# One GLA block, then two diffusion-transformer layers on one core: modulation loads on another queue, two-step ends of the feed-forward's pairs, residuals by tile, a later output step

## The chip, the cores and the metric

The kernel runs on one core of one Trainium2 chip. The metric is the device time of one execution in microseconds (us), the median of several runs. Engine names: PE is TensorE (matmuls, whose weight loads are shown as PEld), DVE is VectorE, ACT is ScalarE, POOL is GpSimd, SP is SyncE, whose queue issues most of the loads from memory.

## What is computed

A first block of 256 tokens of width 1024 (gated linear attention, then a squared-ReLU feed-forward) makes x. Two layers follow on x (the latent tokens) and on 256 context tokens. Each layer takes six modulation vectors from a condition vector: shift, scale and gate for its attention and for its feed-forward. Layer 0 (neighbourhood attention) updates latent and context tokens; layer 1 (grouped-query attention with rotary positions) only the latent ones.

```python
for i in range(DEPTH_2):                       # 2
    ctx_out = i < DEPTH_2 - 1
    mod_l = (silu_c @ ada_w[i] + ada_b[i])[:, None, :]
    mod_c = (silu_cc @ ada_w[i] + ada_b[i])[None, None, :]
    ...
    a_l = ada_norm(h, norm_mix[i], sh1_l, sc1_l)
    a_c = ada_norm(hc, norm_mix[i], sh1_c, sc1_c)
    ...                                        # y_l, y_c: the layer's attention
    h = h + g1_l * y_l
    h = h + g2_l * swiglu_ffn(ada_norm(h, norm_ffn[i], sh2_l, sc2_l), ffn_w_in[i], ffn_w_out[i])
    if ctx_out:
        hc = hc + g1_c * y_c
        hc = hc + g2_c * swiglu_ffn(ada_norm(hc, norm_ffn[i], sh2_c, sc2_c), ffn_w_in[i], ffn_w_out[i])
return rms_norm_2(h, norm_final)

def swiglu_ffn(h, w_in, w_out):
    a, g = jnp.split(h @ w_in, 2, axis=-1)
    return (jax.nn.silu(a) * g) @ w_out
```

The hidden width of the feed-forward is 2816, 22 tiles of 128. `ada_w` of one layer is a matrix of 1024 by 6 x 1024.

## The kernel before

**Weights and products.** Every product is made in about fp32 precision from three matmuls (`mm3`, L213 to L215): each operand is split into a high part, a rounded copy (`wh` or `h`), and a low part, the rest (`wl` or `l`). A weight tile of 128x1024 (512 KB) is loaded by SP's queue into one of five `raw` buffers (`w_load`, L157), then split by ScalarE (copy, L194) and VectorE (subtraction, L195); `wnext` hands out the next one and keeps a few tiles split ahead (`cap`). The order of all weight tiles is the list `UNITS`.

**Modulation.** The products with the condition vector are not made on TensorE. `ada_jobs` (L318) walks over steps, each a 512 KB tile of `ada_w`: it is loaded into one of two buffers `a` (L333) and multiplied and summed along its rows on VectorE with the broadcast condition vector (L353), twice where latent and context tokens both need it. After eight steps GpSimd adds the bias (L368). There are four such walks. `adaC` is the only one with an `order` (the list `STEPS`): its 48 steps cover the feed-forward gate of layer 0 and most of layer 1's modulation, and its steps are taken one or two at a time between the tiles of layer 0's feed-forward (`ada_next`, L1313).

**Layer 0's feed-forward** works on 512 tokens, four token tiles (0 and 1 latent, 2 and 3 context), and on its 22 hidden tiles in four parts (`PARTS`). For each hidden tile f the up products are made, and after each part the down products (`ffn_down0`). Fourteen of the hidden tiles (`SEVEN`) are made as a pair of token halves with seven products in place of eight (`ffn_up7`, L1255): products of sums of tokens (`sT`) with sums of weights. The sums of weights are made while the tile before is worked on (`pair_sums`, L1217, a generator with four pieces; L1230, L1231 split them, L1236 to L1246 add them on VectorE). In `ffn_up7` TensorE accumulates on r, q and g. r is copied out by ScalarE after the first product (L1275), q after the second (L1277), r again after the third (L1284) and after the next product on r (L1291); TensorE may go on accumulating on r only after each copy. `step(cut)` runs the next piece of `pair_sums` behind the copy given.

**The end of a tile.** The last operations on a tile's activations, `end`, are held back if the next tile is a pair, and run in that pair behind the copy of q (L1278 to L1281). For an ordinary tile, `end` splits the product (L1157 on ScalarE, L1158 on VectorE). For a pair it takes silu of the second half (L1305, ScalarE), multiplies (L1306, VectorE) and splits (L1307 ScalarE, L1308 VectorE).

**Down products and residuals.** The last part's down products (`ffn_down0_last`, L1364) are made for half the columns and two token tiles at a time. Then `gated` (L1111) multiplies each of the two tiles by its gate (L1113) and adds it to the residual (L1114), both on VectorE. The squares, the root and the norm of the rows follow (L231 ScalarE, L224 VectorE, L225 GpSimd, L243 VectorE), and the transposes into layer 1 (L258, L271 to L276).

**Layer 1's attention** makes 32 units (16 heads by 2 query tiles), staged: in each step n of the loop one unit is started (scores L1676, L1677) and older ones are moved on (softmax L1682 to L1691, transposes L1695, values L1709). `qfill(n)` (L1728) puts other work between: the rest of the projections and, from `oproj`, one step of the output projection, of its residual and of its transposes. Every n takes one step of `oproj` except n = 29. What is left runs after the loop.

**What sets the order.** At the start and at the end of the kernel the order on some engines is the order written. In between, instructions are put in order when the program is made, by the place in the text and by what is ready; `tc.issue_after(x)` makes the instructions written inside it, on x's engine, follow x. Each engine and queue then works strictly in that order.

Of the kernel before, what the change touches and what calls it, by code (L numbers as in the profile page):

```python
# [15 lines left out]
ALU = mybir.AluOpType  # L16
# [74 lines left out]
def net(ctx, tc, x, xt, small, gk_up, gk_b, g_onorm, wst, final_norm, ctx_in, ctx_t, ada, ada_b, cvec,  # L91
# [226 lines left out]
    def ada_jobs(jobs, order=None):  # L318

        steps = [(L, v, both, k) for L, v, both in jobs for k in range(KD)]  # L320
        if order is not None:
            two, one = [z for z in steps if z[2]], [z for z in steps if not z[2]]
            steps = [(two if n == "2" else one).pop(0) for n in "".join(order)]
            assert not two and not one
        loaded = {}

        def load(n):
            if n < len(steps):
                L, v, _, k = steps[n]
                loaded[n] = sb.tile([P, D], F32, tag="ada", bufs=2, name=nm("a"))  # L330
                if (L, v) == (0, 0) and k < 2:
                    G.tensor_copy(out=loaded[n][:, 0:1], in_=crow[k][:, 0:1])
                nc.sync.dma_start(out=loaded[n], in_=ada[(L * 6 + v) * KD + k])  # L333

        later = []

        def advance():
            for z in list(later):
                if z[0] < site[0]:
                    z[0] = site[0]  # L340
                    if next(z[1], "end") == "end":
                        later.remove(z)

        for n, (L, v, both, k) in enumerate(steps):
            if n == 0:
                load(0)
            load(n + 1)
            raw = loaded.pop(n)
            n_c = 2 if both else 1
            for ci in range(n_c):  # L350
                if k == 0:
                    modc[(L, ci, v)] = const([P, KD], nm("mod"))
                V.tensor_tensor_reduce(out=raw if ci == n_c - 1 else t2([D], BF16), in0=raw, in1=crow[ci], scale=1.0,  # L353
                                       scalar=0.0, op0=ALU.mult, op1=ALU.add,
                                       accum_out=modc[(L, ci, v)][:, k:k + 1])
            if k == KD - 1:
                later.append([site[0], ada_finish(L, v, n_c)])
            yield advance
        while later:
            site[0] += 1  # L360
            advance()
            yield advance
# [748 lines left out]
    def gated(res, acs, L, ci, v, hf):  # L1111
        tmp = t2([512])
        V.tensor_tensor(out=tmp, in0=acs, in1=gates[(L, ci, v, hf)], op=ALU.mult)  # L1113
        V.tensor_tensor(out=res[hf], in0=tmp, in1=res[hf], op=ALU.add)  # L1114

    hc = ctx_tiles()
    run(steps, 100)
# [28 lines left out]
    def ffn_act(pa, pg_, n, hold=False):  # L1146
        a = t2([n])
        A.activation(out=a, in_=pa[:, :n], func=AF.Silu)
        V.tensor_tensor(out=a, in0=pg_[:, :n], in1=a, op=ALU.mult)  # L1149
        if n > S:  # L1150
            h, l = t2([n], F32R), t2([n], F32R)
        else:
            z = t2([2, n], F32R)
            h, l = z[:, 0, :], z[:, 1, :]

        def end():
            A.copy(out=h, in_=a)  # L1157
            V.tensor_tensor(out=l, in0=a, in1=h, op=ALU.subtract)  # L1158

        held_ends.append(end) if hold else end()  # L1160
        return h, l

    def ffn_up(L, src, n, conv=iter(()), hold=False):
# [91 lines left out]
    def ffn_up7(got, conv, hold):  # L1255
        wpos[2] += 2
        r, q, g = [bank()[:, 0:S] for _ in range(3)]
        c1, c2, c3 = t2([2, S]), t2([2, S]), t2([2, S])
        H = KD // 2

        def prod(o, n, c, X, first=True):
            h, l = got[n]
            for j in range(H):
                k = slice(c + j * P, c + (j + 1) * P)
                mm3(o, h[:, k], l[:, k], *X(j), first and j == 0, j == H - 1, not first)

        def step(cut):
            with tc.issue_after(cut.ins):
                run(conv)

        def a(t, j):
            return xs(fT, j, S * t, S)

        prod(r, 0, 0, lambda j: a(0, j))
        A.copy(out=c1[:, 0, :], in_=r)  # L1275
        prod(q, 1, 0, lambda j: sT[(3, j)])
        cut = A.copy(out=c3[:, 0, :], in_=q)  # L1277
        with tc.issue_after(cut.ins):  # L1278
            for end in held_ends:
                end()  # L1280
        held_ends.clear()  # L1281
        step(cut)
        prod(r, 2, 512, lambda j: sT[(2, j)], False)
        cut = A.copy(out=c3[:, 1, :], in_=r)  # L1284
        prod(g, 0, 512, lambda j: a(0, H + j))
        got[0] = None
        V.tensor_tensor(out=c1[:, 0, :], in0=g, in1=c1[:, 0, :], op=ALU.add)
        step(cut)
        prod(r, 2, 0, lambda j: sT[(1, j)], False)
        got[2] = None  # L1290
        cut = A.copy(out=c2[:, 1, :], in_=r)  # L1291
        with tc.issue_after(cut.ins):
            A.activation(out=c1[:, 0, :], in_=c1[:, 0, :], func=AF.Silu)
        V.tensor_tensor(out=c2[:, 1, :], in0=c2[:, 1, :], in1=c3[:, 0, :], op=ALU.add)
        step(cut)
        prod(q, 3, 0, lambda j: a(1, H + j), False)
        V.tensor_tensor(out=c1[:, 1, :], in0=q, in1=c3[:, 1, :], op=ALU.add)
        step(cut)
        prod(r, 1, 512, lambda j: sT[(4, j)], False)
        V.tensor_tensor(out=c2[:, 0, :], in0=r, in1=c1[:, 0, :], op=ALU.mult)  # L1300
        z = c2.rearrange("p t s -> p (t s)")
        h, l = t2([N2], F32R), t2([N2], F32R)

        def end():
            A.activation(out=c1[:, 1, :], in_=c1[:, 1, :], func=AF.Silu)  # L1305
            V.tensor_tensor(out=c2[:, 1, :], in0=c2[:, 1, :], in1=c1[:, 1, :], op=ALU.mult)  # L1306
            A.activation(out=h, in_=z, func=AF.Copy, scale=-1.0)  # L1307
            V.scalar_tensor_tensor(out=l, in0=z, scalar=-1.0, in1=h, op0=ALU.mult, op1=ALU.subtract)  # L1308

        held_ends.append(end) if hold else end()  # L1310
        return h, l

    def ada_next():  # L1313
# [50 lines left out]
    def ffn_down0_last(hf, uu, tiles, between=iter(())):  # L1364
        for f2 in range(0, len(uu), 2):
            u = wnext(("h", "ffn_out0"))
            for i, t in enumerate(tiles):
                for j in range(2):
                    f = f2 + j
                    mm_h(dbank[2 * hf + i], u, j, uu[f], t, False, f == len(uu) - 1, True)  # L1370
                    if f2:
                        run(between)
        for i, t in enumerate(tiles):
            gated((lat + hc)[t], dbank[2 * hf + i], 0, t // 2, 5, hf)

    gq, gkk = const([P, 64], "gq"), const([P, 64], "gkk")
    for g, src in ((gq, q_gain), (gkk, k_gain)):
# [350 lines left out]
    def qfill(n):  # L1728
        run(q1_, 2 if n < 1 else 1)
        run(finish_, 0 if n < 3 else 2 if n < 8 or n % 4 == 0 else 1)  # L1730
        run(oproj_, n != 29)

    def qdone(m):
        head, t = gorder[m]
# [208 lines left out]
```

## Time and profile before

| what | before |
|---|---|
| time, median of 3 runs | 1241.88 us (1241.81 to 1242.5) |
| the profiled execution | 1242.52 us |
| its span, first to last instruction | 1240.7 us |
| mean granted TensorE clock | 0.999 |
| TensorE busy | 1227.8 us, 99% |
| VectorE busy | 987.1 us, 80% |
| ScalarE busy | 753.9 us, 61% |
| GpSimd busy | 78.9 us, 6% |
| weight tiles loaded (SP's queue) | 302 x 512 KB, 4.4 us to landing |
| modulation tiles loaded (SP's queue) | 96 x 512 KB, 4.3 us to landing |

Busy time counts the union of an engine's instructions. A matmul's recorded end lies after the start of the next one, since they are pipelined, so a busy TensorE can hide a short stall; the distance between starts shows it. A line of the waits names the instruction that waited, the one that released it, the time in total, how often, and the longest. In the windows each engine has its busy time and, in brackets, its number of instructions; then come the granted clock, the busy share of the DMA engines and GB/s. In a timeline the first two numbers are start and duration in us, and brackets give idle time ahead of the instruction and what ended it.

### The profile page before, as it was taken

The page shows a single profiled execution, that of the slowest core. Times are in us where ns is not written, and L with a number is a line of the kernel's source. Part 1 is how long each engine was busy: PE and PEld are TensorE (multiplying, and loading weights), DVE is VectorE, ACT ScalarE, POOL GpSimd, SP SyncE. Part 2 cuts the span into 40 slices and gives each one's busy share as a digit, 9 for nine tenths or more (in the row PEclk, how much of TensorE's full clock was granted, in tenths as well). Part 3 has the DMA queues.
Part 4 walks back from the last instruction along what each step waited for, and adds up shares of the span by engine and source line. Part 5 has one row for each costly group of instructions (what it writes and reads, how often), then busy time and mean ns, then how long its engine had stood idle before and what let it go on. Part 6 is the DMA issues. An engine that isn't in the chain of part 4 may idle for free.

```text
span 1240.7 us, 19919 instructions
## 1 busy us (share of the span) xinstructions
PE 1227.8 (99%) x7376; PEld 1056.4 (85%) x7376; DVE 987.1 (80%) x1778; ACT 753.9 (61%) x1490; POOL 78.9 (6%) x137
## 2 busy tenths in 40 slices
PE   9999999999999999999999999999999999999997
PEld 8888898988878777789888988889877777999997
DVE  5968888797989888777998977989888987655555
ACT  8575655666548888745344553645667897644443
POOL 1000000030100000001000000000002320000000
PEclk9999999999999999999999999999999999999999
DMA  8547587887573333483466465566763223755650
GB/s 308 189 155 229 188 296 255 285 265 264 178 272 103 110 109 120 132 268 107 136 232 204 141 225 193 194 201 193 253 236 96 92 86 119 234 187 186 202 177 34
DMA packets 69665, 231.30 MB, mean 186 GB/s; under 512 B 8176, under 2 KB 8864, under 8 KB 69568
## 3 DMA queue, kind: packets, MB, share of 16 engines
q1 hardware_dynamic: 68128, 227.58, 55.7%
q10 hardware_dynamic: 1440, 2.45, 0.5%
q8 instruction: 58, 0.95, 0.3%
q14 instruction: 39, 0.32, 0.1%
HBM read 226.83 MB, written 3.17 MB: 185 GB/s over the span
## 4 chain that ended last, share of the span: by engine, by line
PE 85%; DVE 6%; DMA 4%; ACT 2%; issue 2%; POOL 0%; SPq 0%; POOLq 0%; DVEq 0%
PE b L213 24%; PE b L214 24%; PE b L215 24%; DMA a<-in_ada_dram 3%; PE b L1033 2%; DVE wl L195 1%; PE b L1709 1%; DVE a L353 1%; PE b L1695 1%; PE b L1014 1%; PE b L258 1%; DVE wl L1231 1%; PE b L593 1%; PE b L1676 1%; PE b L995 1%
## 5 line engine op out<-in xcount | busy, mean ns | idle before, releaser
L195 DVE TENSOR_TENSOR wl<-raw,wh 128x1024 fp32r<-128x1024 f32 x272 | 330.4, 1225 | 119.1 <-ACT wh L194 117.5
L194 ACT CAST wh<-raw 128x1024 fp32r<-128x1024 f32 x272 | 284.5, 1052 | 197.9 <-PE b L214 152.5
L213 PE MATMUL b<-t,wh 128*128 128x256 f32 (+1 forms) x1232 | 371.8, 302 | 1.9 <-ACT t L1284 1.9
L214 PE MATMUL b<-t,wl 128*128 128x256 f32 (+1 forms) x1232 | 371.5, 302 | 0.0
L215 PE MATMUL b<-t,wh 128*128 128x256 f32 (+1 forms) x1232 | 371.1, 302 | 0.0
L213 PE MATMUL b<-wh,t 128*128 128x512 f32 (+1 forms) x748 | 298.5, 401 | 0.4 <-ACT t L779 0.3
L215 PE MATMUL b<-wl,t 128*128 128x512 f32 (+1 forms) x748 | 295.2, 395 | 0.0
L214 PE MATMUL b<-wh,t 128*128 128x512 f32 (+1 forms) x748 | 294.7, 394 | 0.0
L213 PEld LDWEIGHTS b<-t,wh 128*128 128x128 f32 x1232 | 231.8, 188 | 14.5 <-ACT t L1284 2.3
L214 PEld LDWEIGHTS b<-t,wl 128*128 128x128 f32 x1232 | 232.1, 188 | 11.9
L215 PEld LDWEIGHTS b<-t,wh 128*128 128x128 f32 x1232 | 231.9, 188 | 10.1 <-DVE t L276 0.2
L215 PEld LDWEIGHTS b<-wl,t 128*128 128x128 f32 x748 | 140.5, 188 | 33.3
L214 PEld LDWEIGHTS b<-wh,t 128*128 128x128 f32 x748 | 140.8, 188 | 30.1 <-issue 0.4
L213 PEld LDWEIGHTS b<-wh,t 128*128 128x128 f32 x748 | 140.4, 188 | 30.5 <-ACT t L779 0.5
L353 DVE CUSTOM_DVE_ANT_0 a<-a,crow 128x1024 f32<-128x1024 f32 x96 | 117.3, 1230 | 14.4 <-DMA a<-in_ada_dram 14.1
L353 DVE CUSTOM_DVE_ANT_0 t<-a,crow 128x1024 bf16<-128x1024 f32 x64 | 78.8, 1236 | 11.3 <-DMA a<-in_ada_dram 11.1
L1230 ACT CAST wh<-raw 128x1024 fp32r<-128x1024 f32 x42 | 43.9, 1049 | 34.2 <-PE b L214 24.5
L1231 DVE TENSOR_TENSOR wl<-raw,wh 128x1024 fp32r<-128x1024 f32 x42 | 50.9, 1216 | 0.6 <-ACT wh L1230 0.5
L368 POOL TENSOR_TENSOR mod<-mod,bcol 128x8 f32<-128x8 f32 x20 | 12.5, 626 | 549.3 <-DVE mod L353 548.1
L225 POOL TENSOR_TENSOR c<-c,mhalf 128x1 f32<-128x1 f32 x21 | 14.6, 697 | 452.1 <-DVE c L224 452.1
L231 ACT ACTIVATE t<-t 128x512 f32<-128x512 f32 x40 | 24.9, 624 | 13.6 <-DVE t L1114 9.1
L1149 DVE TENSOR_TENSOR t<-b,t 128x256 f32<-128x256 f32 (+1 forms) x28 | 14.0, 500 | 20.1 <-PE b L215 18.5
(279 smaller groups left out, 1482.7 us busy)
## 6 DMA issues: line engine op xcount, KB each, us to landing
raw<-in_wst_dram SPq DMA_DIRECT2D x302, 512.0 KB, 4.4
a<-in_ada_dram SPq DMA_DIRECT2D x96, 512.0 KB, 4.3
t<-in_rpb_dram SPq DMA_DIRECT2D x16, 256.0 KB, 4.5
t<-row SPq DMA_DIRECT2D x12, 256.0 KB, 5.9
t<-in_ctx_dram SPq DMA_DIRECT2D x8, 256.0 KB, 6.1
res<-t ACTq DMA_DIRECT2D x8, 256.0 KB, 2.9
t<-res SPq DMA_DIRECT2D x8, 256.0 KB, 7.0
t<-in_xt_dram SPq DMA_DIRECT2D x4, 256.0 KB, 5.1
```

Of the source, the lines that this page charges most:

```text
L194: A.copy(out=h[:, :n], in_=raw[:, :n])
L195: V.tensor_tensor(out=l[:, :n], in0=raw[:, :n], in1=h[:, :n], op=ALU.subtract)
L213: T.matmul(o, lhsT=lh, rhs=rh, start=first, stop=False, skip_group_check=onto)
L214: T.matmul(o, lhsT=ll, rhs=rh, start=False, stop=False, skip_group_check=onto)
L215: T.matmul(o, lhsT=lh, rhs=rl, start=False, stop=last, skip_group_check=onto)
L225: G.tensor_tensor(out=ms[:, 3:4], in0=ms[:, 2:3], in1=mhalf[:, 0:1], op=ALU.pow)
L231: A.activation(out=junk[hf], in_=halves[hf], func=AF.Square, scale=1.0 / 32.0, accum_out=ms[:, hf:hf + 1])
L353: V.tensor_tensor_reduce(out=raw if ci == n_c - 1 else t2([D], BF16), in0=raw, in1=crow[ci], scale=1.0, scalar=0.0, op0=ALU.mult, op1=ALU.add,
L1033: T.matmul(po[e * 64:(e + 1) * 64, cols_], lhsT=v, rhs=probs[(head, "l" if lat_q else "c")][:, c, :], start=(c == 0), stop=(c == n_c - 1))
L1149: V.tensor_tensor(out=a, in0=pg_[:, :n], in1=a, op=ALU.mult)
L1230: A.copy(out=h, in_=r)
L1231: V.tensor_tensor(out=l, in0=r, in1=h, op=ALU.subtract)
```

## The change

Four edits. The loads of `adaC` (the walk with an order) are issued by GpSimd's queue; the other walks stay on SP's. The held ends become generators of two steps: the first runs behind the copy of q as before, the second behind the copy of r that follows (L1284); an ordinary tile's end has nothing in its first step, a pair's end has silu and product in the first and the split in the second. In `ffn_down0_last` each tile's product and sum are written to follow the sum of the tile before. And `qfill` leaves out the steps of `oproj` at n = 28 and n = 30, not at 29.

```diff
@@ -330,7 +330,7 @@
                 loaded[n] = sb.tile([P, D], F32, tag="ada", bufs=2, name=nm("a"))
                 if (L, v) == (0, 0) and k < 2:
                     G.tensor_copy(out=loaded[n][:, 0:1], in_=crow[k][:, 0:1])
-                nc.sync.dma_start(out=loaded[n], in_=ada[(L * 6 + v) * KD + k])
+                (nc.sync if order is None else G).dma_start(out=loaded[n], in_=ada[(L * 6 + v) * KD + k])
@@ -1111,7 +1111,7 @@
     def gated(res, acs, L, ci, v, hf):
         tmp = t2([512])
         V.tensor_tensor(out=tmp, in0=acs, in1=gates[(L, ci, v, hf)], op=ALU.mult)
-        V.tensor_tensor(out=res[hf], in0=tmp, in1=res[hf], op=ALU.add)
+        return V.tensor_tensor(out=res[hf], in0=tmp, in1=res[hf], op=ALU.add)
@@ -1154,10 +1154,11 @@
         def end():
+            yield
             A.copy(out=h, in_=a)
             V.tensor_tensor(out=l, in0=a, in1=h, op=ALU.subtract)
 
-        held_ends.append(end) if hold else end()
+        held_ends.append(end()) if hold else run(end(), 2)
         return h, l
@@ -1277,11 +1278,14 @@
         cut = A.copy(out=c3[:, 0, :], in_=q)
         with tc.issue_after(cut.ins):
             for end in held_ends:
-                end()
-        held_ends.clear()
+                next(end)
         step(cut)
         prod(r, 2, 512, lambda j: sT[(2, j)], False)
         cut = A.copy(out=c3[:, 1, :], in_=r)
+        with tc.issue_after(cut.ins):
+            for end in held_ends:
+                next(end, None)
+        held_ends.clear()
         prod(g, 0, 512, lambda j: a(0, H + j))
@@ -1304,10 +1308,11 @@
         def end():
             A.activation(out=c1[:, 1, :], in_=c1[:, 1, :], func=AF.Silu)
             V.tensor_tensor(out=c2[:, 1, :], in0=c2[:, 1, :], in1=c1[:, 1, :], op=ALU.mult)
+            yield
             A.activation(out=h, in_=z, func=AF.Copy, scale=-1.0)
             V.scalar_tensor_tensor(out=l, in0=z, scalar=-1.0, in1=h, op0=ALU.mult, op1=ALU.subtract)
 
-        held_ends.append(end) if hold else end()
+        held_ends.append(end()) if hold else run(end(), 2)
         return h, l
@@ -1370,8 +1375,10 @@
+        cuts = []
         for i, t in enumerate(tiles):
-            gated((lat + hc)[t], dbank[2 * hf + i], 0, t // 2, 5, hf)
+            with issued_behind(cuts):
+                cuts = [gated((lat + hc)[t], dbank[2 * hf + i], 0, t // 2, 5, hf)]
@@ -1728,7 +1735,7 @@
     def qfill(n):
         run(q1_, 2 if n < 1 else 1)
         run(finish_, 0 if n < 3 else 2 if n < 8 or n % 4 == 0 else 1)
-        run(oproj_, n != 29)
+        run(oproj_, n not in (28, 30))
```

## The prediction

> **What bounds the kernel now.** I read the page first, then who waited for whom on TensorE, then the windows by stage, then the timelines of the places where TensorE stood still, and last the waits around the modulation weights. The page:
>
> ```profile
> span 1240.7 us, 19919 instructions
> PE 1227.8 (99%) x7376; PEld 1056.4 (85%) x7376; DVE 987.1 (80%) x1778; ACT 753.9 (61%) x1490; POOL 78.9 (6%) x137
> ```
>
> The profiled execution took 1242.52 us, 1.8 us of it outside this span; the median of the three timed runs is 1241.88 us, 0.64 us below it. I find every saving in the profile and subtract it from the median. TensorE is busy for all but 12.9 us of the span, so no other engine is the bound as a whole: the only thing that a reordering can win is a place where TensorE stood still. The list of its waits (line that waited, releaser: us in total, times, longest):
>
> ```profile
> PE b L213 <- ACT t L1284: 1.9, 2, 1.5
> ...
> PE b L258 <- DVE t L243: 0.7, 1, 0.7
> PE b L1695 <- DVE t L1691: 0.5, 1, 0.5
> ...
> PE b L258 <- ACT t L271: 0.2, 1, 0.2
> ```
>
> The reader is to see that four entries are all that lies in the stages that the change touches: layer 0's pairs (L1284), the passage from layer 0 to layer 1 (L243, L271) and the end of layer 1's attention (L1691). Together 3.3 us. A stall is a little longer than its entry, since a matmul's recorded end lies behind the start of the next one; I take the true length from the starts. Two of the windows give TensorE's pace (busy us, then count), and the others VectorE's slack (third busy figure):
>
> ```profile
> 340.00:360.00 20.00, 20.00 (x88) 16.07 (x87) 18.27 (x25) 8.30 (x11) 0.00 (x0) 1.00 0.85 291
> ```
> ```profile
> 680.00:720.00 40.00, 40.00 (x341) 39.84 (x340) 36.14 (x59) 25.04 (x47) 0.00 (x0) 1.00 0.48 154
> 720.00:775.00 55.00, 55.00 (x280) 46.24 (x279) 44.40 (x69) 23.25 (x35) 2.82 (x3) 1.00 0.64 210
> ...
> 800.00:836.00 36.00, 36.00 (x173) 29.70 (x172) 30.35 (x48) 15.36 (x26) 1.68 (x3) 1.00 0.62 205
> 836.00:880.00 44.00, 43.64 (x368) 43.35 (x367) 43.87 (x72) 27.10 (x49) 0.59 (x1) 1.00 0.57 180
> ```
>
> A 256-column matmul takes 40.00/341 = 0.117 us and a 512-column one 20.00/88 = 0.227 us, at a granted clock of 1.00. VectorE has 10.6 us to spare in 720 to 775 and 5.7 us in 800 to 836 (both are stretches of down products), but 0.13 us in 836 to 880, the last five pairs. There it is as tight as TensorE.
>
> **Part 1, the pairs' ends in two steps.** One pair (a call of ffn_up7) makes seven products of 12 matmuls, 12 x 0.117 = 1.40 us each. The accumulator r is copied out by ScalarE at L1284, TensorE goes on with product g for 1.40 us, and then needs r again. The first stall, on ScalarE, VectorE and TensorE:
>
> ```profile
> 779.98 0.42 ACT L1305 ACTIVATE t<-t 128x256 f32<-128x256 f32 x1
> 780.30 1.04 ACT L1230 CAST wh<-raw 128x1024 fp32r<-128x1024 f32 x1
> 783.17 0.63 ACT L1307 ACTIVATE t<-t 128x512 fp32r<-128x512 f32 x1 [1.83 <-DVE t L1306]
> 783.71 0.35 ACT L1284 COPY t<-b 128x256 f32<-128x256 f32 x1
> ```
> ```profile
> 781.51 0.69 DVE L1237 TENSOR_TENSOR raw<-raw 128x512 f32<-128x512 f32 x1
> 782.12 0.68 DVE L1240 TENSOR_TENSOR raw<-raw,raw 128x512 f32<-128x512 f32 x1
> 782.72 0.42 DVE L1306 TENSOR_TENSOR t<-t,t 128x256 f32<-128x256 f32 x1
> ```
> ```profile
> 782.35 0.28 PE L215 MATMUL b<-t,wh 128*128 128x256 f32 x1
> 784.12 0.39 PE L213 MATMUL b<-t,wh 128*128 128x256 f32 x1 [1.49 <-ACT t L1284]
> ```
> ```profile
> 847.47 0.28 PE L215 MATMUL b<-t,wh 128*128 128x256 f32 x1
> 848.11 0.39 PE L213 MATMUL b<-t,wh 128*128 128x256 f32 x1 [0.36 <-ACT t L1284]
> ```
>
> The copy L1284 stands on ScalarE behind L1307, the last step of the pair before; L1307 waits for VectorE's L1306, which stands behind the sums of weights (L1237, L1240). So TensorE loses 784.12 - 782.35 - 0.12 = 1.65 us, and by the same reckoning 848.11 - 847.47 - 0.12 = 0.52 us at the second place: 2.17 us. The change puts L1307 behind the copy. ScalarE is free at 780.30 + 1.04 = 781.34, r is done at about 782.47 - 1.40 + 0.28 = 781.35, so the copy ends near 781.7 and TensorE goes on at 782.47 without a stall. What is late next: L1307, still released at 783.14, ends at 783.8; if ScalarE's next weight cast (1.05) goes before the next copy, L1291, that copy ends near 785.2, and TensorE wants it two products after 782.47, at 785.3. That is 0.1 us of room, so I give back 0.2 us: **-2.0 us**, between 0 (the wait only moves) and -2.2.
>
> **Part 2, residuals tile by tile.** Four times gated runs on two tiles; three of them have products behind them. The last one ends layer 0, with TensorE waiting:
>
> ```profile
> 925.23 1.28 DVE L1113 TENSOR_TENSOR t<-b,t 128x512 f32<-128x512 f32 x2
> 926.43 1.28 DVE L1114 TENSOR_TENSOR t<-t,t 128x512 f32<-128x512 f32 x2
> ...
> 928.72 0.88 DVE L243 TENSOR_SCALAR t<-t,c 128x512 f32<-128x512 f32 x2 [0.65 <-POOL c L225]
> 929.51 0.15 DVE L224 SCALAR_TENSOR_TENSOR c<-c 128x1 f32<-128x1 f32 x1
> 930.32 0.88 DVE L243 TENSOR_SCALAR t<-t,c 128x512 f32<-128x512 f32 x2 [0.66 <-POOL c L225]
> ```
>
> Both products (L1113) run before both sums (L1114). One of them alone is 1.28 - 0.60 = 0.68 us. In the new order tile 0's sum ends near 925.23 + 2 x 0.68 + 0.04 = 926.63, not 927.11: 0.48 us sooner; tile 1's ends near 928.0, 0.3 later. The transposes need tile 1, whose second L224 stood behind tile 0's two L243, until 929.51. With tile 0 sooner by 0.48 us it moves to about 929.0, still behind tile 1's own square. So **-0.5 us** of the 0.9 us of waits at L243 and L271, between -0.8 and +0.3 (if VectorE takes tile 1's sum before tile 0's L224, only the delay is left).
>
> **Part 3, output steps.** The filler of the attention now rests once, at step 29; it will rest at 28 and at 30, so that one step more is left for the end. A step is a product of 6 matmuls, 6 x 0.227 = 1.36 us on TensorE, with one weight cast on ScalarE, one subtraction on VectorE and the load of a weight tile some steps ahead on SP's queue, where only weight loads stand at that time. TensorE's only wait there is
>
> ```profile
> 1032.29 0.52 PE L1695 MATMUL b<-cm,t 128*128 128x128 f32 x3 [0.45 <-DVE t L1691]
> ```
>
> The deferred 1.36 us covers it, and VectorE gets to the softmax sooner because the subtraction goes later. The total of work is the same. True length of the wait about 0.6 us; I take **-0.5 us**, between -0.9 and +0.5 (the deferred step pushes the last transposes out, at most by a third of its length, as the held products behind them need not wait).
>
> **Part 4, the loads on GpSimd's queue.** 48 loads of 512 KB leave SP's queue. Waits around them, SP's in 565 to 930 and VectorE's in 720 to 836, and in 565 to 930 the loads' time to landing:
>
> ```profile
> SPq L333 <- DVE mod L353: 133.2, 48, 10.1
> ```
> ```profile
> DVE a L353 <- DMA a<-in_ada_dram: 8.8, 8, 2.6
> DVE t L353 <- DMA a<-in_ada_dram: 5.0, 4, 1.9
> ```
> ```profile
> DMA to landing us min/median/max: 3.5/4.0/6.6
> ```
>
> SP waits 133 us for the two buffers of these loads, and each weight load behind it waits with it; but TensorE's list has no entry that ends in a weight load, so freeing SP wins nothing that the end can see. On the other side, no load from GpSimd's queue is in this trace. What the queue can add is bounded below by nothing and above by GpSimd's own rows:
>
> ```profile
> L225 POOL TENSOR_TENSOR c<-c,mhalf 128x1 f32<-128x1 f32 x21 | 14.6, 697 | 452.1 <-DVE c L224 452.1
> ...
> L220 POOL TENSOR_TENSOR c<-c,mhalf 128x4 f32<-128x4 f32 (+1 forms) x10 | 13.4, 1336 | 0.8
> ```
>
> that is, 0.7 to 1.3 us for an instruction that does almost nothing, so 0 to 1.3 us on each landing. Behind a load that waits for its buffer stand, on GpSimd, the bias sums of the modulation (L368) and, after the last load, the roots (L225); the sums are first used at the end of layer 0's feed-forward, and the roots come after all loads. I take half a microsecond per landing, nearer to the short row. The 12 waits of 720 to 836 then grow by 6 us. VectorE has 10.6 + 5.7 = 16.3 us idle there, 13.8 us of which are these waits already, so 2.5 us are free and 3.5 us have to be hidden by weights that are split up to three tiles ahead (cap is 3) and by an order of VectorE's work that puts splits ahead of sums: **0 us**, from -0.5 (VectorE's waits shrink with SP out of the way) to +5.
>
> The Trainium skill (DMA: Bandwidth & Descriptors, section Latency and other measured facts) speaks against this part: a load issued from GpSimd gets its first byte after about 1 us, one from SP after about 0.6. By it, as an estimate, each landing is 0.4 us later and the sum above stays 0; no run here shows it yet.
>
> **Sum**: -2.0 - 0.5 - 0.5 + 0 = -3.0 us, 1241.9 - 3.0 = 1238.9 us. A measurement of this kernel can tell about 0.2% from no change, 2.5 us, that is from 1239.4 down and from 1244.4 up.
>
> **Rivals.** *The gain is given back in the last pairs.* VectorE is busy for 43.87 of 44 us there. If TensorE arrives 1.65 us earlier and VectorE does not (it is held by the landings before them), the 0.52 us at 848 stays and grows, and L1307, which still waits for L1306, delays ScalarE's casts instead of the copy. Against it: VectorE has 5.7 us idle just before. Then part 1 is worth about 0.7 us, parts 2 and 3 perhaps 0.5 together: 1241.9 - 1.2 = 1240.7 us, no change.
>
> *The loads land late and VectorE becomes the bound.* Place: 800 to 836, where the rows above leave about 5.7 us idle, most of it waits for loads. If each landing is 1.3 us later (the long row of GpSimd), and half of the 12 waits lie there, they grow by 8 us, and VectorE enters the last pairs at least 5 us late with 0.13 us to make it good. TensorE then waits about 5 us, part 1 is lost, parts 2 and 3 keep 1.0: 1241.9 + 5 - 1.0 = 1245.9 us, and 1243.5 us when the lag is half of that. It decides from about 0.6 us per landing, where the 2.5 us and some 5 us of weights split ahead are used up. For it: 12 of the loads in that stretch already end VectorE's idle time. Against it: nothing needs these sums soon, so VectorE's order can put weight splits ahead of them.
>
> *The change does not do what it says*: part 2 fixes only that tile 1's product follows tile 0's sum, not where L224 stands, and part 3 only writes a step down later, while the order of issue follows what is ready; so both may leave the sequence of the work that counts as it is, and part 1 alone is left: 1241.9 - 2.0 = 1239.9 us, just within no change.
>
> **Chances.** Forecast 0.45 (own range 1237.4 to 1239.9, nine tenths of it faster by over 0.2%); given back 0.22; late loads 0.18, of which 0.02 at the near end is inside 0.2%; part 1 alone 0.15, of which 0.02 is below 1239.4. That makes faster 0.40 + 0.02 = 0.42, slower 0.16 and same the other 0.42. The range reaches down to where all waits named here are gone and part 4 wins its 0.5, 1241.9 - 2.2 - 0.9 - 0.9 - 0.5 = 1237.4, taken to 1236.9 for the half microsecond that the runs differ by, and up to the near end of the late loads, 1243.5.
>
> **What would show it.** Right: TensorE has no entry over 0.3 us for the copy L1284; on ScalarE the cast of a pair's result stands behind that copy; on VectorE products and sums of the last residual alternate and TensorE's wait for L243 is below 0.3 us; TensorE has no wait over 0.3 us near 1031; loads of modulation weights come from GpSimd and land within 5 us. Wrong: landings over 5 us with VectorE's waits for them above 25 us in layer 0's feed-forward, or a new entry of TensorE for a weight split there.

## The result

The changed kernel takes 1256.15 us (median of 4 runs, 1255.04 to 1257.59) beside 1242.19 us of the kernel before: a ratio of 1.0114 (95% interval 1.0101 to 1.0126). It is slower by 14.0 us, where 3 us less were forecast, and lies outside the range. The profiled execution took 1255.04 us. Its page:

```profile
span 1253.3 us, 19923 instructions
...
PE 1233.3 (98%) x7376; PEld 1060.7 (85%) x7376; DVE 987.4 (79%) x1778; ACT 754.7 (60%) x1490; POOL 105.5 (8%) x185
```

VectorE's work is the same as before (987.4 us against 987.1). TensorE stands still 7 us longer, and is busy 5.5 us longer with the same matmuls. The list of TensorE's waits:

```profile
PE b L214 <- DVE wl L1232: 6.2, 5, 2.3
...
PE b L213 <- ACT t L1276: 1.3, 1, 1.3
PE b L1702 <- ACT t L1709: 1.2, 1, 1.2
...
PE b L214 <- DVE t L276: 0.3, 1, 0.3
```

The entry for the copy of r (L1284 before, 1.9 us) is gone, as Part 1 promised. In its place stand 6.2 us of waits for VectorE's weight splits in the pairs (L1232), 1.3 us for the copy of r after a pair's first product (L1276), a wait of 1.2 us in layer 1's attention (L1709) and a smaller one at the passage to layer 1 (L276). Where the time comes in can be read from the starts of the matmuls, since both kernels run 7376 of them in the same number per stage: how much later the n-th starts in the changed kernel, at some times of the kernel before:

| time before (us) | 600 | 676 | 705 | 775 | 800 | 880 | 925 | 945 | 1021 | 1045 | 1230 |
|---|---|---|---|---|---|---|---|---|---|---|---|
| later by (us) | -0.6 | +0.6 | +6.4 | +6.5 | +9.0 | +10.5 | +11.6 | +10.6 | +10.5 | +12.0 | +12.0 |

Nearly half comes in one place, 676 to 705, where the first pairs of layer 0's feed-forward begin. VectorE's waits for modulation weights between 565 and 940, before and then after:

```profile
DVE a L353 <- DMA a<-in_ada_dram: 14.1, 15, 2.6
...
DVE t L353 <- DMA a<-in_ada_dram: 8.2, 7, 1.9
```
```profile
DVE a L353 <- DMA a<-in_ada_dram: 23.1, 17, 2.4
...
DVE t L353 <- DMA a<-in_ada_dram: 13.6, 8, 3.3
```

22.3 us became 36.7 us. The windows 600 to 682 and 682 to 706, before and then after, show where this hurts (VectorE's busy time is the third figure, the granted clock the one behind GpSimd's):

```profile
600.00:682.00 82.00, 82.00 (x436) 69.75 (x435) 73.03 (x116) 35.16 (x56) 1.53 (x3) 1.00 0.58 195
682.00:706.00 24.00, 24.00 (x204) 23.84 (x203) 23.45 (x40) 13.30 (x26) 0.00 (x0) 1.00 0.51 165
```
```profile
600.00:682.00 82.00, 81.26 (x429) 68.68 (x428) 65.84 (x106) 33.16 (x53) 12.06 (x21) 1.00 0.55 180
682.00:706.00 24.00, 20.43 (x154) 19.53 (x154) 23.19 (x37) 12.00 (x22) 1.62 (x3) 0.93 0.54 175
```

By 682 VectorE has done 7.2 us less of its work than before, and then come the pairs, where it has nothing to spare: 23.45 of 24 us. One step of it on VectorE, and then TensorE's two longest waits for a weight split:

```profile
679.57 1.23 DVE L353 CUSTOM_DVE_ANT_0 a<-a,crow 128x1024 f32<-128x1024 f32 x1 [1.89 <-DMA a<-in_ada_dram]
...
682.30 1.23 DVE L353 CUSTOM_DVE_ANT_0 a<-a,crow 128x1024 f32<-128x1024 f32 x1 [1.50 <-DMA a<-in_ada_dram]
...
683.45 1.22 DVE L1232 TENSOR_TENSOR wl<-raw,wh 128x1024 fp32r<-128x1024 f32 x1
```
```profile
684.73 0.39 PE L214 MATMUL b<-t,wl 128*128 128x256 f32 x1 [1.79 <-DVE wl L1232]
```
```profile
788.90 0.58 PE L214 MATMUL b<-t,wl 128*128 128x256 f32 x1 [2.30 <-DVE wl L1232]
```

The chain is whole: VectorE waits 1.50 us for a load, sums it, and only then splits the weights that TensorE has been waiting for; 683.45 + 1.22 = 684.67, and TensorE goes on at 684.73. With each of these stalls comes what the prediction did not think of, a drop of the granted clock. Windows of 2 us:

```profile
686.00:688.00 2.00, 1.87 (x9) 1.57 (x8) 2.00 (x4) 1.62 (x4) 0.00 (x0) 0.50 0.63 193
688.00:690.00 2.00, 1.63 (x9) 1.43 (x7) 2.00 (x4) 0.64 (x2) 0.53 (x1) 0.65 0.66 236
788.00:790.00 2.00, 1.10 (x5) 1.10 (x6) 2.00 (x4) 0.79 (x2) 0.53 (x1) 0.60 0.32 88
790.00:792.00 2.00, 2.00 (x12) 2.00 (x12) 1.97 (x5) 0.92 (x2) 0.00 (x0) 0.55 1.03 410
```

The trace has the clock at 0.50 for 3.41 us from 685.99 and again from 788.39; in the kernel before it stands at 1.00 until the end. If TensorE is busy throughout, each drop takes about half of 3.41, 1.7 us: at most some 3.4 us of the 14.

### The profile page after: what moved, and what is told of

It reads as the page before. It is cut to its first block, busy times and chain, and to the rows that moved or that the text cites. A ratio compares the mean times of both kernels' runs of the same rounds, so it can differ in the third digit from the quotient of the medians.

```text
span 1253.3 us, 19923 instructions
## 1 busy us (share of the span) xinstructions
PE 1233.3 (98%) x7376; PEld 1060.7 (85%) x7376; DVE 987.4 (79%) x1778; ACT 754.7 (60%) x1490; POOL 105.5 (8%) x185
## 4 chain that ended last, share of the span: by engine, by line
PE 75%; issue 15%; DVE 4%; DMA 4%; ACT 1%; POOL 1%; POOLq 0%; SPq 0%; DVEq 0%
PE b L213 21%; PE b L214 21%; PE b L215 21%; DMA a<-in_ada_dram 3%; PE b L1033 2%; PE b L1716 1%; PE b L1702 1%; PE b L1014 1%; DVE a L353 1%; POOL a L333 1%; PE b L258 1%; DVE wl L1232 1%; PE b L593 1%; PE b L1683 1%; PE b L995 1%
## 5 line engine op out<-in xcount | busy, mean ns | idle before, releaser
L215 PEld LDWEIGHTS b<-t,wh 128*128 128x128 f32 x1232 | 233.2, 189 | 10.9 <-DVE t L1214 0.8
L333 POOL DMA_DIRECT2D a<-in_ada_dram x48 | 26.0, 543 | 337.8 <-DVE mod L353 334.3
L1232 DVE TENSOR_TENSOR wl<-raw,wh 128x1024 fp32r<-128x1024 f32 x42 | 51.2, 1221 | 0.4 <-ACT wh L1231 0.3
```

Source lines behind the costliest of these rows:

```text
L215: T.matmul(o, lhsT=lh, rhs=rl, start=False, stop=last, skip_group_check=onto)
L333: (nc.sync if order is None else G).dma_start(out=loaded[n], in_=ada[(L * 6 + v) * KD + k])
L1232: V.tensor_tensor(out=l, in0=r, in1=h, op=ALU.subtract)
```

## The experiments

**One part at a time.** Theory A: Part 4 is the cause, through landings that come late. Rival B: the pairs' ends in two steps. Rival C: neither alone. The edits are the hunks of the change: the first run has only this one,

```diff
-                nc.sync.dma_start(out=loaded[n], in_=ada[(L * 6 + v) * KD + k])
+                (nc.sync if order is None else G).dma_start(out=loaded[n], in_=ada[(L * 6 + v) * KD + k])
```

the second all the others, the third only those of the pairs' ends (L1156 to L1310), the fourth only `gated` and `ffn_down0_last`.

> The kernel before with Part 4 alone (48 loads of modulation weights on GpSimd's queue); Parts 1 to 3 left out. Theory A (the loads are the cause: each lands about half a microsecond later, VectorE falls behind, TensorE waits for weight splits of the pairs, and the granted clock halves after the two longest of these waits): 1250 to 1257 us, with entries of TensorE for a weight split in the pairs of over 2 us in all and at least one dip of the clock. Rival B (the pairs' ends in two steps move VectorE's work to where it has no room): 1241 to 1243 us, no such entries. Rival C (neither alone, only both together): 1241 to 1244 us here and in the next run.

Measured: 1255.4 us, ratio 1.0104 (1.0088 to 1.0119).

> Parts 1 to 3 without Part 4 (the 48 loads stay on SP's queue). Theory A: 1239 to 1241.5 us, the clock at 1.00 throughout, TensorE without entries for weight splits in layer 0's pairs. Rival B: 1249 us or more. Rival C: 1241 to 1244 us.

Measured: 1241.76 us, ratio 1.0002 (0.9993 to 1.0012); clock at 1.00, no entry for a weight split. The time misses Theory A's 1241.5 us by 0.3 us: Parts 1 to 3 together save nothing, because Part 3 costs (below).

> Part 1 alone. The prediction's term: 2.0 us less than before, 1240.2 us beside a before of 1242.2; no entry of TensorE for the copy of r over 0.3 us. Rival (the gain is given back in the last pairs): 0.7 us less, 1241.5 us. Rival B: 1249 us or more.

Measured: 1240.07 us, ratio 0.9984 (0.9974 to 0.9993).

> Part 2 alone. The trace of the changed kernel shows the passage from layer 0 to layer 1 about 1 us shorter: by that 1241.2 us beside a before of 1242.2; by the prediction's term 1241.7 us; by the rival (the order of VectorE's work does not change where it counts) 1242.2 us.

Measured: 1242.33 us, ratio 1.0001 (0.9990 to 1.0013).

Part 4 alone makes 13.3 of the 14.0 us, with 6.0 us of waits for weight splits, 3.9 us for the copy of r (1.9 before) and one drop of the clock; rivals B and C fall. VectorE's waits for these loads grow to 23.9 + 12.9 = 36.8 us, about the 36.7 us of the changed kernel. The run also shows how, because VectorE's order of work, which is fixed when the kernel is built, is the same as before up to 657. So each of its instructions can be laid beside the same one before. Sums that waited for a load, before and then with Part 4 alone:

```profile
609.53 1.23 DVE L353 CUSTOM_DVE_ANT_0 a<-a,crow 128x1024 f32<-128x1024 f32 x1 [0.21 <-DMA a<-in_ada_dram]
...
644.41 1.23 DVE L353 CUSTOM_DVE_ANT_0 a<-a,crow 128x1024 f32<-128x1024 f32 x1 [0.53 <-DMA a<-in_ada_dram]
...
655.77 1.23 DVE L353 CUSTOM_DVE_ANT_0 t<-a,crow 128x1024 bf16<-128x1024 f32 x1 [1.29 <-DMA a<-in_ada_dram]
...
661.86 1.23 DVE L353 CUSTOM_DVE_ANT_0 t<-a,crow 128x1024 bf16<-128x1024 f32 x1 [1.31 <-DMA a<-in_ada_dram]
```
```profile
611.81 1.23 DVE L353 CUSTOM_DVE_ANT_0 a<-a,crow 128x1024 f32<-128x1024 f32 x1 [2.15 <-DMA a<-in_ada_dram]
...
648.29 1.23 DVE L353 CUSTOM_DVE_ANT_0 a<-a,crow 128x1024 f32<-128x1024 f32 x1 [2.28 <-DMA a<-in_ada_dram]
...
661.00 1.23 DVE L353 CUSTOM_DVE_ANT_0 t<-a,crow 128x1024 bf16<-128x1024 f32 x1 [2.08 <-DMA a<-in_ada_dram]
...
669.80 1.23 DVE L353 CUSTOM_DVE_ANT_0 t<-a,crow 128x1024 bf16<-128x1024 f32 x1 [3.53 <-DMA a<-in_ada_dram]
```

The lag is 2.3 us, then 3.9, 5.2 and 7.9 us (about 7.5 at the first pairs). It does not grow evenly, by half a microsecond per load, but in steps at a few loads. The first step, as the queues saw it, before and then with Part 4 alone:

```profile
603.92 1.47 SPq L333 DMA_DIRECT2D a<-in_ada_dram  x2
606.20 1.57 SPq L157 DMA_DIRECT2D raw<-in_wst_dram  x2
```
```profile
606.53 1.56 SPq L157 DMA_DIRECT2D raw<-in_wst_dram  x2
```
```profile
604.52 0.53 POOL L333 DMA_DIRECT2D a<-in_ada_dram  x1 [12.42 <-DVE mod L353]
605.66 0.53 POOL L333 DMA_DIRECT2D a<-in_ada_dram  x1 [0.62 <-DVE mod L353]
```

Before, the second load was issued near 605.07 (the second of the two in the first row) and was summed at 609.53, 4.46 us later, with two weight loads behind it in the same queue. From GpSimd it was issued at 605.66 and summed at 611.81, 6.15 us later: 1.7 us more, while the same two weight loads ran beside it from another queue. Two explanations are left: A1, a load from GpSimd is issued later by itself; A2, two queues share the DMA engines, and a weight load no longer stands behind the load that is urgent.

**Which queue carries what.** The next two runs put the weights of layer 0's feed-forward on GpSimd's queue, without and with the modulation weights:

```diff
-            nc.sync.dma_start(out=raw, in_=wst[SLOT[UNITS[wpos[0]]]])
+            (G if UNITS[wpos[0]][1].endswith("0") else nc.sync).dma_start(out=raw, in_=wst[SLOT[UNITS[wpos[0]]]])
```

> The kernel before, with the other loads moved: the weights of layer 0's feed-forward (w_load) go on GpSimd's queue and the 48 loads of modulation weights stay on SP's. So two queues load at the same time, as in the changed kernel, but the modulation weights are issued by SP, 0.04 us after their buffer comes free. Theory A1 (what hurts is the late issue from GpSimd, 0.26 us later and 0.2 us longer): 1240 to 1244 us. Theory A2 (what hurts is that a weight load no longer stands behind the modulation load in one queue and takes half of the DMA engines from it): 1248 to 1257 us, with landings of modulation weights of 5 to 7 us.

Measured: 1248.04 us, ratio 1.0044 (1.0029 to 1.0059); landings at 3.4 to 6.1 us after the issue, against 3.5 to 6.6 us in the kernel before. Landings of 5 to 7 us, which A2 named, are no more frequent than there, among those that the traces give.

> Both the weights of layer 0's feed-forward and the 48 loads of modulation weights on GpSimd's queue: one queue as in the kernel before, but issued from GpSimd. A1 (late issue): 1249 to 1257 us, landings at 4.1 us after the release at best as in the run with Part 4 alone. A2 (two queues at once): 1240 to 1245 us, few landings over 5 us.

Measured: 1253.38 us, ratio 1.0086 (1.0071 to 1.0101), in the range of A1.

Neither theory stands alone, and the two times can't be compared as they are: part of each arises at the program's end. There GpSimd runs a last instruction called DRAIN, the longest of three in these rows (in ns); before, then with the weights on GpSimd, then in a later run whose 48 modulation loads are issued by GpSimd in two pieces each:

```profile
L1939 POOLq DRAIN  x3: 39/78/646, 1235.9 to 1240.5; - x3
```
```profile
L1939 POOLq DRAIN  x3: 40/102/6552, 1238.3 to 1245.4; - x3
```
```profile
L1944 POOLq DRAIN  x3: 40/102/8512, 1250.1 to 1259.1; - x3
```

It takes 0.65 us where GpSimd has issued no load, 4.59 us after 48 loads, 6.55 after 72 and 8.51 after 96, but 1.81 us after 120 (both kinds on its queue); why so few there is not known. From the issue of the last output to the end of the span pass 3.5, 4.0, 6.0, 7.9 and 3.7 us. So 2.5 us of the 5.7 us that the first of these runs costs stand at the end, and in its trace TensorE itself is 2.4 us later than before at 1230; the 1248.04 us reach A2's range only with the end. In the second run, which costs 11.0 us, TensorE is 11.7 us later, though there is one queue for both kinds of load. Of the 13.3 us of Part 4 alone, 0.5 us stand at the end.

VectorE's order is nearly the same in both runs, and its lag at the first pairs is about 3.5 and 6.9 us. It comes from the modulation loads here too: between 600 and 682 VectorE waits for them, before and then with the weights alone on GpSimd,

```profile
DVE a L353 <- DMA a<-in_ada_dram: 3.7, 6, 0.9
DVE t L353 <- DMA a<-in_ada_dram: 3.2, 3, 1.3
```
```profile
DVE a L353 <- DMA a<-in_ada_dram: 8.9, 7, 2.3
DVE t L353 <- DMA a<-in_ada_dram: 2.7, 3, 1.3
```

that is 6.9 us, then 11.6 us, and 13.8 us with both kinds on GpSimd; no engine waits for a weight load there. GpSimd's own rows explain part of the second run:

```profile
641.99 0.53 POOL L333 DMA_DIRECT2D a<-in_ada_dram  x1 [2.61 <-DVE mod L353]
642.51 0.53 POOL L157 DMA_DIRECT2D raw<-in_wst_dram  x1
```
```profile
648.32 1.22 DVE L353 CUSTOM_DVE_ANT_0 a<-a,crow 128x1024 f32<-128x1024 f32 x1 [3.42 <-DMA a<-in_ada_dram]
```

This load took 6.3 us to its sum with a weight load right behind it in its own queue; on SP the same pair, issued at 640.72 and 641.14, let the sum start at 644.41, 3.7 us later. One such place is no rule, so how much of the 11.7 us is a late issue and how much sharing stays open. The Trainium skill (DMA: Bandwidth & Descriptors, Queues, rings and completion order) states the rule for two queues: each DMA engine takes turns between the queues that have work for it, packet by packet. The run with the weights alone on GpSimd agrees as far as it goes (the urgent loads are issued by SP as before, and VectorE's waits for them rise from 6.9 to 11.6 us); the trace shows when loads land, not whose packet an engine served.

**A third buffer.** `bufs=2` becomes `bufs=3` for the modulation weights and `NT2 = 58` becomes 56, with Part 4 alone and without it.

> Part 4 alone with three buffers for the modulation weights instead of two (and 56 instead of 58 temporary tiles, to make room). Theory A (VectorE is late because it waits for landings): a third buffer hides 4 us of landing, VectorE's waits for the loads fall from above 30 us to below 12, and the time is 1239 to 1244 us. If VectorE is late for another reason (GpSimd's instructions in its way, for one): 1252 us or more.

Measured: 1251.95 us, ratio 1.0076 (1.0060 to 1.0093).

> The kernel before with three buffers for the modulation weights and 56 temporary tiles, loads on SP's queue: the control for the run before. All theories: 1240 to 1243 us; 1 to 2 us of it faster than before if VectorE's 22 us of waits for these loads are what makes the stalls on the copy of r.

Measured: 1241.18 us, ratio 0.9991 (0.9982 to 1.0001).

```profile
DVE a L353 <- DMA a<-in_ada_dram: 23.3, 17, 4.6
...
DVE t L353 <- DMA a<-in_ada_dram: 1.0, 3, 0.4
```

The first expectation failed: with Part 4 the waits fell to 24.3 us, not below 12, and the cost only from 13.3 to 9.6 us. The time is that of the other expectation, 1252 us, by which VectorE would be late for another reason than the landings. The waits speak against that reason: they are 10.6 us more than the 13.7 us of the control, which is 10.8 us faster, and VectorE's busy time had not grown in the changed kernel (987.4 against 987.1 us). A load from GpSimd can come late with three buffers as well (the longest wait is even 4.6 us), and the order that is built with three buffers has two sums more ahead of the first pairs (64 against 62), which must be paid for there when they are late.

**Part 3 alone, and a late issue alone.** In the second of these runs each load stays on SP but is split, so that its bulk is issued one SP instruction later:

```diff
+                    nc.sync.dma_start(out=loaded[n][:, 0:16], in_=src[:, 0:16])
+                    nc.sync.dma_start(out=loaded[n][:, 16:], in_=src[:, 16:])
```

> Part 3 alone (output steps 28 and 30 rest instead of 29). The prediction's term: 0.5 us less, 1241.8 us beside a before of 1242.3. What the run of Parts 1 to 3 leaves for it, since Part 1 alone took off 2.1 and Part 2 alone nothing: 1.0 to 1.7 us more, 1243.3 to 1244 us, with an entry of TensorE of 1.2 us for the step L1709 near 1030.

Measured: 1243.18 us, ratio 1.0008 (0.9999 to 1.0018).

> The kernel before with each of the 48 loads of modulation weights split on SP's queue: 16 columns first, then the other 1008. Both wait for the same buffer, so the bulk is issued one SP instruction (0.33 us) later, and nothing else changes: one queue, hardware descriptors, GpSimd not involved. A1 (a late issue by itself is dear, because two buffers make a chain of landings): VectorE 4 to 7 us late at the last loads before the first pairs, 1247 to 1254 us. If what made the run with both kinds of load on GpSimd slow is something else of GpSimd's: 1242 to 1244.5 us.

Measured: 1241.21 us, ratio 0.9999 (0.9989 to 1.0008); VectorE waits 13.7 + 8.1 = 21.8 us for these loads.

A1 in its simple form falls: a later issue of a third of a microsecond in SP's undivided queue costs nothing here. But the build had arranged VectorE's work differently here, with one sum fewer ahead of the first pairs. So a theory D came up: what hurts is an order that is made for earlier landings.

**Two candidates.**

> A candidate: Part 1 with three buffers for the modulation weights and 56 temporary tiles, all loads on SP. If the two savings add up (2.1 and 1.2 us): 1239.0 us; if the third buffer saves the same stalls as Part 1: 1240.2 us. Faster than both kernels either way.

Measured: 1240.14 us, ratio 0.9983 (0.9975 to 0.9992): the third buffer saves the same stalls as Part 1.

> Parts 1 and 2. By the sum of the two runs alone (2.1 less and 0.2 more): 1240.3 us. If Part 2's gain at the passage to layer 1 (1 us in the trace) stays while its loss at the passage to the second half goes: 1239.3 us.

Measured: 1241.28 us, ratio 0.9993 (0.9984 to 1.0002): neither value; part of Part 1's gain is lost again.

**The order against the lateness.** The same split with the loads on GpSimd, then Part 1 with the split on SP, then the weights on GpSimd with the split on SP:

> Part 4 alone with each of the 48 loads on GpSimd's queue split into 16 columns and 1008, as in the run with the split on SP. In that run the order that was fixed for VectorE when the kernel was built has one more sum fewer ahead of the first pairs (61 against 62 at the second result of the first pairs), and the same here. Theory A1 (each landing is late, by about 0.5 us from GpSimd and by one more DMA instruction here): 1255 to 1262 us. Theory D (VectorE's fixed order is made for durations that the loads on SP keep and those from GpSimd don't; an order that leaves them more time takes the loss away): 1242 to 1248 us.

Measured: 1262.03 us, ratio 1.0162 (1.0148 to 1.0176), at the upper end of A1's range; 4.5 us of the cost stand at the program's end, in the DRAIN shown above.

> A candidate: Part 1 with the split loads on SP. If the gains add up (2.1 us and 0.1): 1239.9 us; if the looser order of VectorE also takes away the 1.3 us that TensorE waits for a weight split in the last pairs of Part 1 alone: 1238.6 us.

Measured: 1241.92 us, ratio 0.9999 (0.9990 to 1.0008): a miss, Part 1's gain is gone in this order.

> The weights of layer 0's feed-forward on GpSimd's queue with the modulation weights split on SP: two queues at once, order of VectorE with more room. D: most of the 5.7 us that two queues cost is gone, 1242 to 1244.5 us. A2 (sharing the DMA engines costs by itself): 1247 us or more.

Measured: 1252.56 us, ratio 1.0082 (1.0068 to 1.0096), as A2 expects; 2.5 us of the cost stand at the program's end.

Theory D falls twice. In the order that gave 1241.2 us with everything on SP, moving nothing but the weight loads to GpSimd costs 11.3 us, 9.0 of them on TensorE in the trace, and moving the modulation weights instead costs 20.8 us, 16.1 of them on TensorE. VectorE's order differs from that run's in a few neighbours only, and it is again about 7 us late at the first pairs with the modulation weights on GpSimd; its waits for them between 600 and 682 are 5.2 us with everything on SP, 13.4 and 14.8 us in these two runs. So the lateness of the modulation loads is the cause in every slow version, and loads in two queues at once are enough to bring it about. They are not needed for it, as the run with both kinds on GpSimd's queue shows.

## Why the prediction was wrong

**Part 1 was right in mechanism, and its size fits in part by luck.** Predicted -2.0 us, measured alone -2.06 (interval -3.2 to -0.9). TensorE no longer waits for the copy L1284 in the pairs. But the 1.9 us of the one trace that the term was read from are not a fixed price: the runs with Part 2 alone and Part 3 alone have the pairs as before, and TensorE waits 0.7 and 1.4 us at this copy. And in two more builds, Parts 1 and 2 and Part 1 with the split loads, most of the gain or all of it is missing. The trace of the run with Part 1 alone also shows the rival "given back in the last pairs" at work in small:

```profile
854.11 0.39 PE L214 MATMUL b<-t,wl 128*128 128x256 f32 x1 [0.91 <-DVE wl L1232]
```

At 848 TensorE has gained 2.5 us on the kernel before, at 856 only 1.2 are left. That execution took 1241.42 us, the longest of its ten, so most runs keep more.

**Part 2 was mis-sized: -0.5 predicted, nothing measured.** The order did change where it counts: in the run with Part 2 alone the passage to layer 1 near 930 is 1.0 us shorter. But the call that ends the first half, near 910 to 920, pays it back, and the prediction had said of that call only that products stand behind it:

```profile
919.50 0.50 PE L214 MATMUL b<-wh,t 128*128 128x512 f32 x1 [0.26 <-DVE t L276]
```

There TensorE loses the same 1.0 us, since VectorE's L276 for the transposed tiles, which feed these very products, come later.

**Part 3 had the wrong sign: -0.5 predicted, about +1.2 measured alone** (its interval, -0.1 to +2.2 us, just reaches zero; the trace has TensorE 1.4 us later there). It removed the wait for L1691 and made a longer one. ScalarE and TensorE in the run with Part 3 alone:

```profile
1031.52 1.07 ACT L194 CAST wh<-raw 128x1024 fp32r<-128x1024 f32 x1
1032.45 0.68 ACT L1702 COPY t<-b 128x256 f32<-128x256 f32 x2
```
```profile
1033.18 0.63 PE L1695 MATMUL b<-cm,t 128*128 128x128 f32 x4 [1.16 <-ACT t L1702]
```

The copy that the last transposes need stands behind a weight cast of the filler. In the kernel before, cast and copy have the same order (1031.09 and 1032.03), but the transposes at 1032.29 went ahead without that copy. The prediction counted the filler's cast among its work but looked only at VectorE for who would be late; ScalarE's queue is where the step hurts.

**Part 4 is the step that failed: 0 us, from -0.5 to +5, against +13.3 alone.** The prediction let VectorE's waits for these loads grow by 6 us, in 720 to 836 alone, and hid them in idle time and in splits made ahead; with Part 4 alone they grew by 14.5 us (22.3 to 36.8 between 565 and 940), VectorE came to the first pairs 7.5 us late, and TensorE waited. Landings over 5 us, waits above 25 us and an entry of TensorE for a weight split are what the prediction itself named as signs of being wrong. Four things in it were wrong.
- *The price of a landing.* "0 to 1.3 us on each landing" was bounded by GpSimd's short instructions, as if only the issue could cost. The loads of the changed kernel between 565 and 930 (the durations are in ns):

```profile
L333 POOL DMA_DIRECT2D a<-in_ada_dram x46: 527/528/607, 589.5 to 840.6; - x46
...
DMA to landing us min/median/max: 3.7/3.9/7.2
```

  The DMA instruction takes 0.53 us against 0.33 on SP, and it starts 0.30 us after the buffer's release against 0.04. The quickest load is 3.7 + 0.30 = 4.0 us from release to landing against 3.5 + 0.04, so 0.5 us later, the value that was taken. Most of the lag comes in steps of 0.6 to 2.8 us at a few loads: with Part 4 alone 15 of these 46 landed more than 5 us after the release. The two slowest of 600 to 682 there, issued at 605.66 and 638.82, took 6.1 and 6.9 us, each with two weight loads issued on SP within the next 2.1 us; the load ahead of the step to 7.9 us took 5.0 us and met one weight load and the next modulation load.
- *SP's wait.* The 133 us that SP waited for the two buffers were read as a hindrance that nobody feels. In SP's one queue they also kept each weight load behind the modulation load that VectorE wanted next; now weights with buffers to spare run beside a load with none. How much of the 13.3 us this makes was not shown: with two queues and the modulation loads on SP TensorE came 2.4 and 9.0 us late in two builds, with both kinds in GpSimd's one queue, where the weight loads stand behind again, 11.7 us.
- *The place.* The waits were weighed in 720 to 836. The lag arises in 600 to 682, where before VectorE had 9 us idle, 6.9 of them already these waits; that leaves 2 us, and the pairs that follow have less than one. The two stretches were not one reserve either: 7 of the 12 waits, 10.4 of 10.6 us idle, lie in 720 to 775 and only 5, 3.3 us, in 800 to 836, where the rival of late loads speaks of 12.
- *The way out.* "An order of VectorE's work that puts splits ahead of sums" does not come about by itself: the order is fixed at the build, and with Part 4 alone it was the same as before until 657, when VectorE was already 5 us late.

The rival of late loads named the mechanism and the entry for a weight split, but priced it at 1.6 to 4 us with the place in 800 to 836, and had no drop of the clock. The Trainium skill (DMA: Bandwidth & Descriptors, Latency and other measured facts) has a load from GpSimd about 0.4 us later at its first byte. The 0.5 us of the quickest loads agree with that, but it is not the whole: two queues at once made TensorE 2.4 and 9.0 us late with the modulation weights issued from SP.

**The sum of the parts.** -2.1 + 0.2 + 1.2 + 13.3 = 12.6 us alone, 14.0 together. The remaining 1.4 us are not resolved: the interval of Part 4 alone by itself reaches from 10.9 to 14.8 us. The second drop of the clock does not explain them either, since of the two profiled executions the one with two drops (changed kernel, 1255.04 us) is the faster, and the one with Part 4 alone (1255.67 us) has one. Of all versions, Part 1 alone (1240.07 us) and Part 1 with a third buffer (1240.14 us) are the ones that are faster than the kernel before by more than their intervals.

## What to carry to other kernels

A queue in which a transfer waits for a buffer also holds back the transfers behind it; before a load is moved to a queue of its own, ask what will then run beside it, whether the moved load is the urgent one, and what the new issuing engine still has to do when the program ends (here up to 4.5 us). Where a chain of load, work and release has two buffers and its consumer runs in a fixed order, sum the consumer's idle time in the stretch just ahead of the tightest stage, not on the average. And when work is deferred, look at every engine that the deferred step uses: a copy behind a cast on ScalarE cost more than the wait that was removed.

## What the runs showed of the hardware

The granted clock can fall with stalls of little more than 2 us, but does not always. Of ten single stalls of TensorE between 2.08 and 3.50 us in the profiled runs, seven brought a clock of 0.50 for 3.41 us, from 2.2 to 3.8 us after the stall's start, and three (2.14, 2.15 and 3.24 us) did not; none of the single stalls between 1.5 and 1.91 us did, but two stalls of 1.58 and 0.50 us within 2.3 us did. (A stall is here the distance of two matmul starts.) The length alone does not decide. The Trainium skill (TensorE: Matmul & The Clock Gate, HAM oscillation) warns of gaps over about 3.4 us; here 2.1 us could be enough. Its Part 1 says that activity is watched in free-running windows of about 3.4 us, and the 3.41 us of each drop and the unequal fate of like stalls agree with that.

GpSimd's last DRAIN grows by 0.08 us for each load that it has issued (4.59, 6.55 and 8.51 us for 48, 72 and 96 loads), but is 1.81 us after 120; up to 4.5 us of it lengthen the kernel, although the last of these loads was issued over 340 us before the end.

Landings scatter from trace to trace: in the kernel before one load near 735 took 6.6 us, in the run with Part 1, at nearly the same moment, 4.2 us. And 25 runs of the kernel before spread from 1239.8 to 1245.5 us, so a change of a few tenths of a per cent can only be judged from many runs.
